# Joining the value products of two query tiles in a differential attention, with feature-major outputs and moved weight and gate splits

## The chip, the cores and the metric

The kernel runs on one core of a Trainium2 chip. The metric is the device time of one execution in microseconds. A core has a matrix engine (TensorE, PE in the profile, with its weight loads as PEld), a vector engine (VectorE, DVE), an engine for activations (ScalarE, ACT), a general one (GpSimd, POOL) and one that issues transfers (SP). Each takes its instructions in the order of its own queue and waits where an operand or a buffer isn't ready.

## What is computed

The reference is a block of two layers over 1024 latent tokens with 256 context tokens, 1024 features. The even layer has a Fourier mixer and a differential attention side by side, the odd layer a gated short convolution. The part that the change is about is the attention of the even layer and what follows it:

```python
def one_block(qblk):
    s = jnp.einsum('bqhmd,bkhmd->bhmqk', qblk, k,
                   preferred_element_type=jnp.float32) * ATTN_SCALE
    p = jax.nn.softmax(s, axis=-1)
    a = p[:, :, 0] - lam * p[:, :, 1]
    return jnp.einsum('bhqk,bkhv->bqhv', a.astype(v.dtype), v)
...
ao = (rms_norm(attn_o, subln_g) * (1.0 - lam_init)).reshape(b, n, ATT_WIDTH)
y = jnp.concatenate([fo, ao], axis=-1) * jax.nn.silu(proj[..., G0:])
return y @ w_out
```

There are 4 heads, each with two score maps over 1280 keys (context and latent), and values of 128 features. `rms_norm` divides by the root of the mean square over the 128 features of a token's output; a softmax's denominator that is common to both maps can be left out ahead of it, as long as the small constant in the norm is scaled with its square.

## The kernel before

All of it runs with the matrix engine as the main worker. Products that must be more exact than one pass are split: an operand is cast to a rounded high part (ScalarE) and the rest is subtracted as a low part (VectorE or POOL), and three products are summed.

**Projections** (lines 598 to 667). Tokens are taken in tiles of 128; `proj_tok` makes 24 records of 128x512 for one of them. `wnext(n)` splits the next n weight tiles (line 185, with `whalf`, lines 171 and 172) and asks for the next raw ones. Only TensorE's order is written out by hand in this stage; the other engines' is found by a scheduler.

**Fourier mixer and gates** (lines 749 to 953, TensorE and VectorE in written order). `fft_a(g)` makes the sequence transform of group g and splits its results (`split`, lines 744 and 746); `fft_b` transforms over channels and writes `fo` (line 789). Between them stand the gates' products. `tpart` makes split copies of `tk` for the gates in `arena`: line 885 is the high part on ScalarE, line 888 the low part on VectorE, and lines 866 and 867 first complete `tk` for the later quarters.

**Attention** (lines 1157 to 1205, all engines in written order). The 32 steps i are query tiles of 128 for (head, tile). For each of the two maps a score goes to its own three banks (S0, S1; lines 1025 and 1026); VectorE takes the row maximum (`rowmax`, line 1030), ScalarE the exponential with its row sum (`expo`, line 1041). `combine(i - 1)` forms p0 + cc * p1, 1024 keys on VectorE (line 1055), 256 on POOL (lines 1052, 1053). `turn(i - 2, c)` transposes up to four key blocks into a bank and ScalarE copies them out as `aT` (line 1067). `values(i - 2)` sums ten products with aT as the stationary operand and 128 value features as the moving one, so that the output lies token-major (line 1075); VectorE copies it to `o` (line 1084) and ScalarE sums its squares per token (line 1090).

Four tiles are a group g. `fin_a` has POOL turn the sums into 1/root (lines 1096 to 1100, the power at 1100) and scale `o` (1101). `fin_b` transposes the four outputs (1109), VectorE applies gain and gate to `y` (1111), ScalarE casts the high part (1113) and POOL subtracts for the low part (1115).

PSUM has eight banks. S0 and S1 hold six; the two others are the pool `pst` with its tag "t": `ps_t` (a turn), `ps_av` (values) and `ps_o` (outputs) take them in turn, and whoever comes next waits until the readers of the one before the last are done.

**End of the attention** (lines 1190 to 1205). The last two tiles' turns and values are put between the steps of the first output projections (`proj_feat2(W[0], 0)`, then W[1]; `at={k: ...}` names what goes ahead of step k; one step is three records of 512 columns).

Of the kernel before, what the change touches and what calls it, by code (L numbers as in the profile page):

```python
# [17 lines left out]
P = 128  # L18
# [19 lines left out]
def block_kernel(tc, A):  # L38
# [44 lines left out]
    ones_dv = const.tile([P, 1], F32, name="ones_dv")  # L83
    nc.vector.memset(ones_dv, 1.0 / P)
# [533 lines left out]
    for tt in range(NTC, NK):  # L618
        if tt == NTC + 1:
            wnext(2)  # L620
# [128 lines left out]
    def fft_a(g):  # L749
# [4 lines left out]
        for i in range(4):  # L754
# [303 lines left out]
    def turn(i, c):  # L1058

        n = min(4, NK - 4 * c)  # L1060
        pt = pst.tile([P, NB], F32, name="ps_t", tag="t", bufs=2)
        p0 = tiles[i, 0][0]
        for j in range(n):
            k = 4 * c + j
            nc.tensor.transpose(pt[:, j * P:(j + 1) * P], p0[:, k * P:(k + 1) * P], ident)  # L1065
        at = av.tile([P, NB], F32, name="aT", bufs=4)
        nc.scalar.copy(out=at[:, :n * P], in_=pt[:, :n * P])
        groups[i, c] = at

    def values(i):  # L1070
        g, j = divmod(i, 4)
        v = preps[i // 8][2]
        ps = pst.tile([P, NB], F32, name="ps_av", tag="t", bufs=2)[:, :P]
        for k in range(NK):
            nc.tensor.matmul(ps, lhsT=groups[i, k // 4][:, (k % 4) * P:(k % 4 + 1) * P],  # L1075
                             rhs=v[:, k * P:(k + 1) * P], start=k == 0, stop=k == NK - 1)
# [7 lines left out]
        nc.vector.tensor_copy(out=o[:, j, :], in_=ps)

    def squares(i):
        g, j = divmod(i, 4)
        o, ss, _ = groups[g, "f"]
        sq = av.tile([P, P], F32, name="osq", bufs=1)
        nc.scalar.activation(out=sq, in_=o[:, j, :], func=AF.Square, accum_out=ss[:, j:j + 1])  # L1090

    def fin_a(g, eng=nc.gpsimd):

        o, ss, _ = groups[g, "f"]
        z0 = z0s.pop(g)
        nc.gpsimd.tensor_tensor(out=z0, in0=z0, in1=z0, op=ALU.mult)
        nc.gpsimd.tensor_scalar(out=z0, in0=z0, scalar1=EPS, scalar2=None, op0=ALU.mult)
        nc.gpsimd.tensor_scalar(out=ss, in0=ss, scalar1=1.0 / DV, scalar2=None, op0=ALU.mult)
        nc.gpsimd.tensor_tensor(out=ss, in0=ss, in1=z0, op=ALU.add)
        nc.gpsimd.tensor_tensor(out=ss, in0=ss, in1=mhalf[:, 0:4], op=ALU.pow)  # L1100
        eng.tensor_tensor(out=o, in0=o, in1=ss.unsqueeze(2).broadcast_to([P, 4, P]), op=ALU.mult)

    def fin_b(g):

        f, half = NH + g // 2, g % 2
        o, _, sg = groups.pop((g, "f"))
        pt = pst.tile([P, NB], F32, name="ps_o", tag="t", bufs=2)
        for j in range(4):
            nc.tensor.transpose(pt[:, j * P:(j + 1) * P], o[:, j, :], ident)
        y = av.tile([P, NB], F32, name="y", bufs=1)  # L1110
        nc.vector.scalar_tensor_tensor(out=y, in0=pt, scalar=g08, in1=sg, op0=ALU.mult, op1=ALU.mult)
# [45 lines left out]
    for i in range(NQ):  # L1157
        if i % 8 == 0 and i // 8 + 1 < NH:
            loads = att_prep(i // 8 + 1, nc.sync)
        if i % 8 > 1:  # L1160
            for _ in range(min(3, len(loads))):
                loads.pop(0)()
        score(i, 0)
        if i >= 2:
            turn(i - 2, 0)
            turn(i - 2, 1)
# [3 lines left out]
        if i >= 3:  # L1170
            squares(i - 3)
        if i >= 6 and i % 4 == 2:
            fin_a((i - 6) // 4)
# [6 lines left out]
        if i >= 2:  # L1180
            values(i - 2)
        if i >= 7 and i % 4 == 3:
            fin_b((i - 7) // 4)
# [14 lines left out]
    pend = [proj_feat2(W[0], 0, {1: lambda: turn(NQ - 2, 2), 2: lambda: values(NQ - 2), 4: lambda: turn(NQ - 1, 0),  # L1198
                                 5: lambda: (turn(NQ - 1, 1), squares(NQ - 2)), 7: lambda: turn(NQ - 1, 2)})]
    values(NQ - 1)  # L1200
    squares(NQ - 1)
    fin_a(NG - 1, nc.vector)
    pend.append(proj_feat2(W[1], 0))
# [558 lines left out]
```

## Time and profile before

| what | us |
|---|---|
| median of 3 runs | 1080.52 (1079.1 to 1081.81) |
| the profiled execution | 1081.25 |
| its span | 1079.4 |
| attention, from the first exponential of the first tile to that of the last | 371.62 to 554.74 |
| busy: PE, DVE, ACT, POOL | 1031.8, 760.0, 480.7, 436.8 |

The profile comes from one execution. Its span reaches from the first to the last instruction of the program; the execution's time has something around it. Durations of matrix records overlap with those of their neighbours, so their pace is read from starts or from the chain of waits, which follows what ended last back from the end of the program. In the timeline a row's end tells in brackets how long the engine was idle before it and what ended that.

### The profile page before, as it was taken

The numbers are of one execution on the slowest core, as the hardware profiler recorded it, in microseconds if no ns is written. First come the engines' busy times: TensorE is split into PE (matmuls) and PEld (weight loads), VectorE is DVE, ScalarE is ACT, GpSimd is POOL, SyncE is SP. The second block draws the span as 40 slices with busy tenths as digits, with TensorE's granted clock in tenths as the row PEclk, the third lists the DMA queues.
The fourth block names the chain that finished last, engine by engine and source line by source line (L and its number), as shares of the span: only waits on it lengthen the run. The fifth ranks groups of instructions, "written<-read, shape, count | busy, mean of one in ns | idle before, by whom it ended". The sixth has DMA issues, their size and how long they took to land.

```text
span 1079.4 us, 14123 instructions
## 1 busy us (share of the span) xinstructions
PE 1031.8 (96%) x5128; PEld 843.3 (78%) x5128; DVE 760.0 (70%) x1112; ACT 480.7 (45%) x876; POOL 436.8 (40%) x379
## 2 busy tenths in 40 slices
PE   6989999989999899999999999999999999998898
PEld 3667888878887699899988878777888888786676
DVE  4599956957888288888873386996555554579953
ACT  4453234312445377777763363634333333343420
POOL 1257115530454047775666644034443543402031
PEclk9999999999999999999999999999999999998999
DMA  9823896354111987081004643021112111113421
GB/s 335 339 97 117 253 370 225 108 152 136 43 61 66 249 196 177 25 190 52 18 21 156 198 156 134 0 78 60 59 39 75 43 60 59 59 39 107 145 99 58
DMA packets 61380, 131.12 MB, mean 121 GB/s; under 512 B 5248, under 2 KB 30208, under 8 KB 58112
## 3 DMA queue, kind: packets, MB, share of 16 engines
q1 hardware_dynamic: 60240, 125.64, 36.7%
q0 software_dynamic: 1072, 4.59, 1.2%
q8 instruction: 40, 0.66, 0.3%
q14 instruction: 28, 0.23, 0.1%
HBM read 105.57 MB, written 24.64 MB: 121 GB/s over the span
## 4 chain that ended last, share of the span: by engine, by line
PE 64%; DVE 21%; POOL 4%; ACT 4%; issue 3%; DMA 3%; SPq 0%; ACTq 0%; POOLq 0%; DVEq 0%
PE psX L657 6%; PE psX L659 6%; PE psX L658 6%; PE ps_av L1075 5%; PE ps_tok L284 3%; PE ps_tok L285 3%; PE ps_tok L286 3%; PE psY L658 3%; PE psY L659 3%; PE psY L657 3%; PE S L1025 3%; PE S L1026 3%; DVE nm L1030 2%; PE ps_t L1065 2%; DMA ada_raw<-in_ada_dram 2%
## 5 line engine op out<-in xcount | busy, mean ns | idle before, releaser
L284 PE MATMUL ps_tok<-whi,hhi 128*128 128x512 f32 x288 | 118.0, 410 | 2.5 <-ACT hhi L393 1.5
L285 PE MATMUL ps_tok<-whi,hlo 128*128 128x512 f32 x288 | 115.0, 399 | 3.5 <-DVE hlo L397 3.5
L286 PE MATMUL ps_tok<-wlo,hhi 128*128 128x512 f32 x288 | 114.8, 399 | 0.6 <-DVE wlo L172 0.4
L634 POOL TENSOR_TENSOR s<-wraw 128x512 f32<-128x512 f32 x20 | 26.7, 1333 | 212.5 <-DMA wraw<-in_wodd_dram 101.7
L1030 DVE TENSOR_REDUCE nm<-S 128x1 f32<-128x1280 f32 x64 | 95.2, 1487 | 22.0 <-PE S L1026 17.2
L1041 ACT ACTIVATE p<-S,nm 128x1280 f32<-128x1280 f32 x64 | 85.1, 1330 | 44.7 <-DVE nm L1030 40.9
L61 ACT CAST wop<-wraw 128x512 fp32r<-128x512 f32 x106 | 65.2, 619 | 82.7 <-PE ps_feat L1130 22.0
L657 PE MATMUL psX<-B,wop 128*128 128x512 f32 x240 | 95.6, 398 | 5.0 <-ACT u L1366 2.5
L659 PE MATMUL psX<-B,wop 128*128 128x512 f32 x240 | 95.3, 397 | 4.3 <-DVE wop L1312 4.3
L658 PE MATMUL psX<-B,wop 128*128 128x512 f32 x240 | 94.8, 395 | 0.0
L62 POOL TENSOR_TENSOR wop<-wraw,wop 128x512 fp32r<-128x512 f32 x52 | 71.5, 1377 | 42.1 <-ACT wop L61 42.0
L1075 PE MATMUL ps_av<-v,aT 128*128 128x128 f32 x640 | 76.8, 276 | 0.0
L1075 PEld LDWEIGHTS ps_av<-v,aT 128*128 128x128 f32 x640 | 74.2, 192 | 0.2
L285 PEld LDWEIGHTS ps_tok<-whi,hlo 128*128 128x128 f32 x288 | 55.1, 191 | 16.8 <-DVE hlo L397 6.0
L284 PEld LDWEIGHTS ps_tok<-whi,hhi 128*128 128x128 f32 x288 | 55.3, 192 | 16.2 <-issue 2.2
L1052 POOL TENSOR_TENSOR p<-p,cc 128x256 f32<-128x256 f32 x32 | 40.3, 1259 | 64.7 <-DVE cc L1049 45.1
L286 PEld LDWEIGHTS ps_tok<-wlo,hhi 128*128 128x128 f32 x288 | 55.1, 191 | 13.1 <-DVE wlo L172 1.4
L658 PE MATMUL psY<-B,wop 128*128 128x512 f32 x160 | 63.6, 397 | 1.7 <-DVE B L1259 1.7
L659 PE MATMUL psY<-B,wop 128*128 128x512 f32 x160 | 63.5, 397 | 0.0
L657 PE MATMUL psY<-B,wop 128*128 128x512 f32 x160 | 63.5, 397 | 0.0
L657 PEld LDWEIGHTS psX<-B,wop 128*128 128x128 f32 x240 | 45.1, 188 | 18.3 <-ACT u L1366 3.4
L659 PEld LDWEIGHTS psX<-B,wop 128*128 128x128 f32 x240 | 45.0, 188 | 17.0 <-DVE wop L1312 6.2
(354 smaller groups left out, 2694.5 us busy)
## 6 DMA issues: line engine op xcount, KB each, us to landing
ada_raw<-in_ada_dram SPq DMA_DIRECT2D x24, 1024.0 KB, 7.6
wraw<-in_wodd_dram SPq DMA_DIRECT2D x32, 512.0 KB, 3.5
wraw<-in_wo_dram SPq DMA_DIRECT2D x24, 512.0 KB, 4.1
wraw<-in_wtok_dram SPq DMA_DIRECT2D x16, 512.0 KB, 5.3
arena<-kd SPq DMA_DIRECT2D x16, 320.0 KB, 9.0
kq<-kd SPq DMA_DIRECT2D x16, 320.0 KB, 10.2
xt<-in_xT_dram SPq DMA_DIRECT2D x16, 256.0 KB, 6.3
xr<-in_xT_dram SPq DMA_DIRECT2D x16, 256.0 KB, 4.0
```

What stands on the lines that cost most here:

```text
L61: nc.scalar.copy(out=o[:, 0, :], in_=src)
L62: eng.tensor_tensor(out=o[:, 1, :], in0=src, in1=f32(o[:, 0, :]), op=ALU.subtract)
L284: nc.tensor.matmul(ps, lhsT=hh, rhs=whi, start=k == 0, stop=False)
L285: nc.tensor.matmul(ps, lhsT=hl, rhs=whi, start=False, stop=False)
L286: nc.tensor.matmul(ps, lhsT=hh, rhs=wlo, start=False, stop=k == KT - 1)
L657: nc.tensor.matmul(ps, lhsT=a, rhs=x[k][0], start=start and k == 0, stop=False, skip_group_check=not start)
L658: nc.tensor.matmul(ps, lhsT=a, rhs=x[k][1], start=False, stop=False, skip_group_check=not start)
L659: nc.tensor.matmul(ps, lhsT=b, rhs=x[k][0], start=False, stop=k == 3, skip_group_check=not start)
L1030: nc.vector.tensor_reduce(out=nm, in_=S[m][:, :NKEY], op=ALU.max, axis=AX.X, negate=True)
L1041: nc.scalar.activation(out=p, in_=S[m][:, :NKEY], func=AF.Exp, bias=tiles.pop((i, m, "nm")), accum_out=z)
L1052: nc.gpsimd.tensor_tensor(out=p1[:, ks], in0=p1[:, ks], in1=c.broadcast_to([P, POOLK]), op=ALU.mult)
L1075: nc.tensor.matmul(ps, lhsT=groups[i, k // 4][:, (k % 4) * P:(k % 4 + 1) * P], rhs=v[:, k * P:(k + 1) * P], start=k == 0, stop=k == NK - 1)
```

## The change

1. **Two tiles in one product.** With i odd, a = i - 3 is the first of two tiles that are handled together; in the next, even step a is the same. `turn(a, c)` transposes key blocks 2c and 2c + 1 of both tiles into one bank; five turns make 512 columns each. `values(a, keys)` has the values as the stationary operand and 256 columns of aT as the moving one, so the output is feature-major, 128 features by 256 tokens. Turns 0 and 1 stand in the odd step behind the first score, turns 2 and 3 behind the second; turn 4 and key blocks 0 to 3 in the even step behind the first score, blocks 4 to 9 behind the second. The last two tiles' turns and values stand in the first output projection.
2. **Norm and gate, feature-major.** `outputs` has VectorE scale by the gain, a number for each partition now, and ScalarE square, both out of PSUM, for two tiles at once. `fin_z` and `fin_a` (POOL) do the small constant and the gate. `fin_m` sums squares over features with four one-column products, `fin_d` makes 1/root and a diagonal of it, `fin_r` spreads it over all partitions with a product of 512 columns, and `fin_b` multiplies. The gain now carries the root of 128 in place of a mean.
3. **Weight splits.** `wnext(2)` in the query loop becomes `wnext(1)` at two tiles.
4. **Gates' low parts.** In the last `fft_a` the first quarter's `tpart` goes ahead of the splits.
5. A constant that nothing read is gone.

The diff, without renamed comments and blank lines:

```diff
-        nc.vector.tensor_scalar(out=g08, in0=small[:, S_SUB:S_SUB + 1], scalar1=1.0 - LAM0, scalar2=None,
+        nc.vector.tensor_scalar(out=g08, in0=small[:, S_SUB:S_SUB + 1], scalar1=(1.0 - LAM0) * DV ** 0.5, scalar2=None,
...
-        if tt == NTC + 1:
-            wnext(2)
+        if tt in (NTC + 1, NTC + 3):
+            wnext(1)
...
-    def fft_a(g):
+    def fft_a(g, then=None):
...
+        if then:
+            then()
         ch, cl = split(fev, pc, NB, "gc", 1)
...
-    cur = fft_a(3)
+    qs = [quarter_of(t) for t in arena]
+    cur = fft_a(3, lambda: tpart(qs[0], range(4)))
     gate_product(1, 1)
     gop(1, 2)
-    qs = [quarter_of(t) for t in arena]
-    tpart(qs[0], range(4))
     fft_b(*cur)
...
+    def turn(a, c):
         pt = pst.tile([P, NB], F32, name="ps_t", tag="t", bufs=2)
+        for n in range(4):
+            k, p0 = 2 * c + n // 2, tiles[a + n % 2, 0][0]
+            nc.tensor.transpose(pt[:, n * P:(n + 1) * P], p0[:, k * P:(k + 1) * P], ident)
+        at = av.tile([P, NB], F32, name="aT", bufs=5)
+        nc.scalar.copy(out=at, in_=pt)
+    def values(a, keys):
+        v = preps[a // 8][2]
+        if keys[0] == 0:
+            groups[a, "ps"] = pst.tile([P, NB], F32, name="ps_av", tag="t", bufs=2)[:, :2 * P]
+        for k in keys:
+            nc.tensor.matmul(groups[a, "ps"], lhsT=v[:, k * P:(k + 1) * P],
+                             rhs=groups[a, k // 2][:, (k % 2) * 2 * P:(k % 2 + 1) * 2 * P], start=k == 0,
+                             stop=k == NK - 1)
+    def outputs(a):
...
+        nc.vector.tensor_scalar(out=o[:, qs], in0=ps, scalar1=g08, scalar2=None, op0=ALU.mult)
+        nc.scalar.activation(out=sq[:, qs], in_=ps, func=AF.Square)
+    def fin_z(g):
+        z0 = z0s[g]
+        nc.gpsimd.tensor_tensor(out=z0, in0=z0, in1=z0, op=ALU.mult)
+        nc.gpsimd.tensor_scalar(out=z0, in0=z0, scalar1=EPS * DV, scalar2=None, op0=ALU.mult)
     def fin_a(g, eng=nc.gpsimd):
+        o, _, sg = groups[g, "f"]
+        eng.tensor_tensor(out=o, in0=o, in1=sg, op=ALU.mult)
+    def fin_m(g):
+        ps, sq, z0 = pst.tile([P, NB], F32, name="ps_m", tag="t", bufs=2)[:, :4], groups[g, "f"][1], z0s.pop(g)
+        for j in range(4):
+            nc.tensor.matmul(ps[:, j:j + 1], lhsT=sq[:, j * P:(j + 1) * P], rhs=ones[:, 0:1], start=True, stop=True)
+    def fin_d(g):
+        nc.vector.tensor_tensor(out=z0, in0=ps, in1=z0, op=ALU.add)
+        nc.gpsimd.tensor_tensor(out=z0, in0=z0, in1=mhalf[:, 0:4], op=ALU.pow)
+        dg = groups[g, "d"] = av.tile([P, 4, P], F32, name="dg", bufs=1)
+        nc.gpsimd.tensor_tensor(out=dg, in0=ident.unsqueeze(1).broadcast_to([P, 4, P]),
+                                in1=z0.unsqueeze(2).broadcast_to([P, 4, P]), op=ALU.mult)
+    def fin_r(g):
+        ps = groups[g, "r"] = pst.tile([P, NB], F32, name="ps_o", tag="t", bufs=2)
+        nc.tensor.matmul(ps, lhsT=ones, rhs=groups.pop((g, "d")).rearrange("p j d -> p (j d)"), start=True, stop=True)
     def fin_b(g):
+        nc.vector.tensor_tensor(out=y, in0=groups.pop((g, "r")), in1=y, op=ALU.mult)
...
+        odd, a = i % 2, i - 3 - (i + 1) % 2
         score(i, 0)
+        if a >= 2 and odd:
+            outputs(a - 2)
+        if a >= 0 and odd:
+            turn(a, 0)
+            turn(a, 1)
+        elif a >= 0:
+            turn(a, 4)
+            values(a, range(0, 4))
         rowmax(i, 0)
...
         score(i, 1)
+        if a >= 0 and odd:
+            turn(a, 2)
+            turn(a, 3)
+            if a >= 4 and a % 4 == 0:
+                fin_m((a - 4) // 4)
+            elif a >= 6:
+                fin_r((a - 6) // 4)
+        elif a >= 0:
+            values(a, range(4, NK))
         rowmax(i, 1)
+        if a >= 4 and a % 4 == 0 and odd:
+            fin_d((a - 4) // 4)
+        if a >= 6 and a % 4 == 2 and odd:
+            fin_b((a - 6) // 4)
         expo(i, 1)
...
+    turn(NQ - 4, 4)
+    values(NQ - 4, range(NK))
+    fin_r(NG - 2)
+    fin_b(NG - 2)
+    outputs(NQ - 4)
     combine(NQ - 1)
+    pend = [proj_feat2(W[0], 0, {2: lambda: turn(NQ - 2, 0), 3: lambda: turn(NQ - 2, 1),
+                                 4: lambda: turn(NQ - 2, 2), 5: lambda: turn(NQ - 2, 3),
+                                 6: lambda: turn(NQ - 2, 4)})]
+    values(NQ - 2, range(NK))
+    outputs(NQ - 2)
     fin_a(NG - 1, nc.vector)
+    pend.append(proj_feat2(W[1], 0, {2: lambda: (fin_m(NG - 1), fin_d(NG - 1)), 7: lambda: fin_r(NG - 1)}))
```

How the instructions stand now is shown at three places. First ScalarE in the attention, before: one step, with `p0` and `p1` the exponentials of the two maps, `aT` the copies of turned weights, `osq` the squares.

```order
L1067 COPY aT_3375<-ps_t_3370 128x512
L1067 COPY aT_3382<-ps_t_3377 128x512
L1090 ACTIVATE osq_3392,ss_3294<-o_3293 128x128
L1041 ACTIVATE p0_3394,z0_3395<-S0_3166,nm0_3384 128x1280
L1067 COPY aT_3406<-ps_t_3403 128x256
L1041 ACTIVATE p1_3410,z1_3411<-S1_3167,nm1_3408 128x1280
```

And the same place now, an odd step and the even one behind it:

```order
L1089 ACTIVATE osq_3388<-ps_av_3459 128x256
L1064 COPY aT_3506<-ps_t_3501 128x512
L1064 COPY aT_3513<-ps_t_3508 128x512
L1040 ACTIVATE p0_3524,z0_3349<-S0_3164,nm0_3515 128x1280
L1064 COPY aT_3537<-ps_t_3532 128x512
L1064 COPY aT_3544<-ps_t_3539 128x512
L1040 ACTIVATE p1_3557,z1_3558<-S1_3165,nm1_3551 128x1280
L1064 COPY aT_3571<-ps_t_3566 128x512
L1040 ACTIVATE p0_3586,z0_3587<-S0_3164,nm0_3578 128x1280
L1040 ACTIVATE p1_3603,z1_3604<-S1_3165,nm1_3601 128x1280
```

The odd step has four copies now, two of them behind its first exponential, and the even step one.

Second, TensorE in the same steps, before, without the records of the scores (`ps_t` a turn, `ps_av` the values, `ps_o` the output's transposes):

```order
L1065 MATMUL ps_t_3853<-cst_78,p0_3736 128x128 x4
L1065 MATMUL ps_t_3860<-cst_78,p0_3736 128x128 x4
...
L1065 MATMUL ps_t_3885<-cst_78,p0_3736 128x128 x2
L1075 MATMUL ps_av_3895<-v1_3168,aT_3858 128x128 x4
L1075 MATMUL ps_av_3895<-v1_3168,aT_3865 128x128 x4
L1075 MATMUL ps_av_3895<-v1_3168,aT_3888 128x128 x2
L1109 MATMUL ps_o_3907<-cst_78,o_3567 128x128 x4
```

Now, from the second score of an odd step to the first values of the even one, again without the scores; of each turn only the first transpose of each tile is shown:

```order
L1062 MATMUL ps_t_3532<-cst_78,p0_3348 128x128
L1062 MATMUL ps_t_3532<-cst_78,p0_3415 128x128
...
L1062 MATMUL ps_t_3539<-cst_78,p0_3348 128x128
L1062 MATMUL ps_t_3539<-cst_78,p0_3415 128x128
...
L1106 MATMUL ps_m_3546<-ones_80,osq_3388 128x1
...
L1062 MATMUL ps_t_3566<-cst_78,p0_3348 128x128
L1062 MATMUL ps_t_3566<-cst_78,p0_3415 128x128
...
L1073 MATMUL ps_av_3573<-aT_3506,v0_2076 128x256 x2
L1073 MATMUL ps_av_3573<-aT_3513,v0_2076 128x256 x2
```

The third bank that an odd step asks for behind its first turns is now that of ps_m (or ps_o), ahead of the next step's first score.

Third, VectorE at the end of the attention, before, from the last maximum (`o<-ps_av` the output copies, `y` a group's output, `p` the combination, `x` an output of W[0]):

```order
L1030 TENSOR_REDUCE nm_5234<-S_3167 128x1
L1084 COPY o<-ps_av 128x128
L1111 SCALAR_TENSOR_TENSOR y<-ps_o,g_102,sga 128x512
L1048 RECIPROCAL cc<-z_5237 128x1
L1049 SCALAR_TENSOR_TENSOR cc<-cc,neglam,z_5031 128x1
L1055 SCALAR_TENSOR_TENSOR p_5221<-p_5236,cc,p_5221 128x1024
```

And now:

```order
L1111 TENSOR_TENSOR z_4546<-ps_m,z_4546 128x4
L1125 TENSOR_TENSOR o<-ps_o,o 128x512
L1088 TENSOR_SCALAR o<-ps_av,g_100 128x256
L1047 RECIPROCAL cc<-z_4973 128x1
L1048 SCALAR_TENSOR_TENSOR cc<-cc,neglam,z_4774 128x1
L1054 SCALAR_TENSOR_TENSOR p_4939<-p_4972,cc,p_4939 128x1024
```

The last tile's combination stands behind the output of group 6, which needs `fin_r`, and behind the outputs of tiles 28 and 29.

More of the change, by code (lines that the diff above doesn't have):

```diff
@@ L82, in block_kernel @@
     nc.vector.memset(mhalf, -0.5)
-    ones_dv = const.tile([P, 1], F32, name="ones_dv")
-    nc.vector.memset(ones_dv, 1.0 / P)
     xs = [[None] * KT for _ in range(2)]
@@ L1056, in combine @@
                                        op1=ALU.add)
-    def turn(i, c):
-        n = min(4, NK - 4 * c)
+    def turn(a, c):
         pt = pst.tile([P, NB], F32, name="ps_t", tag="t", bufs=2)
[L1062 to L1076, printed above, removed]
+        for n in range(4):
+            k, p0 = 2 * c + n // 2, tiles[a + n % 2, 0][0]
+            nc.tensor.transpose(pt[:, n * P:(n + 1) * P], p0[:, k * P:(k + 1) * P], ident)
@@ new lines, in turn @@
+        at = av.tile([P, NB], F32, name="aT", bufs=5)
+        nc.scalar.copy(out=at, in_=pt)
+        groups[a, c] = at
+    def values(a, keys):
[6 more added lines that the diff above has]
+                             stop=k == NK - 1)
@@ L1077, in values @@
+    def outputs(a):
+        g, j = divmod(a, 4)
         if j == 0:
-            o = av.tile([P, 4, P], F32, name="o", bufs=2)
-            ss = av.tile([P, 4], F32, name="ss", bufs=2)
+            o = av.tile([P, NB], F32, name="o", bufs=2)
+            sq = av.tile([P, NB], F32, name="osq", bufs=1)
             sg = av.tile([P, NB], F32, name="sga", bufs=2)
             nc.sync.dma_start(out=sg, in_=sgd[g // 2, :, (g % 2) * NB:(g % 2 + 1) * NB])
-            groups[g, "f"] = [o, ss, sg]
-        o, ss, _ = groups[g, "f"]
@@ L1084, in values @@
[L1084 to L1090, printed above, removed]
-    def fin_a(g, eng=nc.gpsimd):
[L1094 to L1101, printed above, removed]
+            groups[g, "f"] = [o, sq, sg]
@@ new lines, in outputs @@
+        o, sq, _ = groups[g, "f"]
+        ps, qs = groups.pop((a, "ps")), slice(j * P, (j + 2) * P)
+        nc.vector.tensor_scalar(out=o[:, qs], in0=ps, scalar1=g08, scalar2=None, op0=ALU.mult)
[4 more added lines that the diff above has]
+        nc.gpsimd.tensor_scalar(out=z0, in0=z0, scalar1=EPS * DV, scalar2=None, op0=ALU.mult)
+    def fin_a(g, eng=nc.gpsimd):
+        o, _, sg = groups[g, "f"]
+        eng.tensor_tensor(out=o, in0=o, in1=sg, op=ALU.mult)
@@ L1103, in fin_b @@
+    def fin_r(g):
+        ps = groups[g, "r"] = pst.tile([P, NB], F32, name="ps_o", tag="t", bufs=2)
+        nc.tensor.matmul(ps, lhsT=ones, rhs=groups.pop((g, "d")).rearrange("p j d -> p (j d)"), start=True, stop=True)
     def fin_b(g):
         f, half = NH + g // 2, g % 2
[L1106 to L1110, printed above, removed]
@@ L1111, in fin_b @@
-        nc.vector.scalar_tensor_tensor(out=y, in0=pt, scalar=g08, in1=sg, op0=ALU.mult, op1=ALU.mult)
+        y, _, _ = groups.pop((g, "f"))
+        nc.vector.tensor_tensor(out=y, in0=groups.pop((g, "r")), in1=y, op=ALU.mult)
         yh = yao.tile([P, NB], F32R, name="yh", tag="y", bufs=16)
@@ L1169, in block_kernel @@
             combine(i - 1)
[L1170 to L1173, printed above, removed]
+        if a >= 4 and a % 4 == 0 and odd:
+            fin_a((a - 4) // 4)
+        if a >= 2 and a % 4 == 2 and not odd:
+            fin_z((a - 2) // 4)
         expo(i, 0)
         score(i, 1)
-        if i >= 2:
-            turn(i - 2, 2)
+        if a >= 0 and odd:
[7 more added lines that the diff above has]
+            values(a, range(4, NK))
         rowmax(i, 1)
+        if a >= 4 and a % 4 == 0 and odd:
+            fin_d((a - 4) // 4)
+        if a >= 6 and a % 4 == 2 and odd:
+            fin_b((a - 6) // 4)
         expo(i, 1)
[L1180 to L1183, printed above, removed]
         if i == 4:
@@ L1189, in block_kernel @@
             fo_split(*fo, i // 4 - 2, nc.gpsimd)
-    turn(NQ - 2, 0)
-    turn(NQ - 2, 1)
+    turn(NQ - 4, 4)
[3 more added lines that the diff above has]
+    outputs(NQ - 4)
     combine(NQ - 1)
-    squares(NQ - 3)
+    fin_z(NG - 1)
     cls("sco")
@@ L1197, in block_kernel @@
     y0(0)
[L1198 to L1201, printed above, removed]
+    pend = [proj_feat2(W[0], 0, {2: lambda: turn(NQ - 2, 0), 3: lambda: turn(NQ - 2, 1),
[3 more added lines that the diff above has]
+    outputs(NQ - 2)
     fin_a(NG - 1, nc.vector)
-    pend.append(proj_feat2(W[1], 0))
+    pend.append(proj_feat2(W[1], 0, {2: lambda: (fin_m(NG - 1), fin_d(NG - 1)), 7: lambda: fin_r(NG - 1)}))
     w0next(eng=nc.vector)
```

5 lines of the change are left out of this document (2 added, 3 removed).

## The prediction

> **What bounds the kernel now.** I read the page's first part, then the attention stage in windows and in the chain of waits, because nearly all edits lie there. First the page's engine totals and the row of the stage in the view by windows (busy us, instructions, granted clock, DMA share, GB/s).
>
> ```profile
> PE 1031.8 (96%) x5128; PEld 843.3 (78%) x5128; DVE 760.0 (70%) x1112; ACT 480.7 (45%) x876; POOL 436.8 (40%) x379
> 388.50:554.70 166.20, 163.69 (x1202) 151.45 (x1201) 142.85 (x175) 125.89 (x264) 104.86 (x116) 1.00 0.38 94
> ```
>
> TensorE is busy 98% of this stage at full clock. VectorE, at 86%, has some slack. So the question is what TensorE gets to do, and whether it then has to wait. The chain (start, us, what) has one query tile in it:
>
> ```profile
> 498.67 0.23 PE S L1025
> ...
> 499.71 0.12 PE S L1026
> 499.83 0.87 PE ps_t L1065 x8
> ...
> 501.86 0.22 PE ps_t L1065 x2
> 502.08 2.23 PE ps_av L1075 x20
> 504.31 0.23 PE S L1025
> ```
>
> A score is 4x0.23 + 2x0.12 = 1.16 us; with eight transposes, the second score, two transposes and the 20 records of the value product the tile takes 504.31 - 498.67 = 5.64 us. Where VectorE and ScalarE end last, the chain reads so:
>
> ```profile
> 488.00 0.13 PE S L1026
> ...
> 488.23 1.49 DVE nm L1030
> ...
> 490.08 1.74 DVE p L1055
> 491.81 1.41 DVE nm L1030
> ...
> 493.31 0.95 ACT p L1041
> ...
> 494.78 0.50 PE S L1025
> ```
>
> From the end of a score, 488.13, its maximum starts 0.10 later and lasts 1.49; the weights' combination starts 1.85 after that start and lasts 1.74 here (1.28 elsewhere in the chain, with POOL quiet); the second maximum, 1.41, ends at 493.22, the exponential starts at 493.31, and the next score in that bank starts 1.47 later. The starts of the first exponentials give the real pace (timeline; the rows are those of tiles 1, 2, 3, 7 and 31):
>
> ```profile
> 377.21 1.33 ACT L1041 ACTIVATE p<-S,nm 128x1280 f32<-128x1280 f32 x1 [1.28 <-DVE nm L1030]
> 382.51 1.35 ACT L1041 ACTIVATE p<-S,nm 128x1280 f32<-128x1280 f32 x1
> 388.52 1.32 ACT L1041 ACTIVATE p<-S,nm 128x1280 f32<-128x1280 f32 x1
> 411.95 1.33 ACT L1041 ACTIVATE p<-S,nm 128x1280 f32<-128x1280 f32 x1
> 554.74 1.33 ACT L1041 ACTIVATE p<-S,nm 128x1280 f32<-128x1280 f32 x1
> ```
>
> From tile 7 to tile 31 it is 142.79 / 24 = 5.95, so **11.90 us for two tiles**, of which 11.28 are the work above and 0.22 a group's output transposes.
>
> **The change, part by part.** What do the new TensorE operations cost? A stream of 256-column f32 records is not in the trace. Its neighbours are (TensorE's timeline, start and us; then the row of line 228 with ns min/median/max, and the page's group of the value products, busy us and mean ns):
>
> ```profile
> 137.90 0.39 PE L286 MATMUL ps_tok<-wlo,hhi 128*128 128x512 f32 x1
> 138.13 0.95 PE L591 MATMUL ps_col<-ones,ada_sum 128*128 128x1 f32 x8
> 139.25 0.39 PE L285 MATMUL ps_tok<-whi,hlo 128*128 128x512 f32 x1
> 624.15 0.39 PE L1130 MATMUL ps_feat<-yh,wop 128*128 128x512 f32 x1
> 624.38 1.02 PE L228 MATMUL ps_r<-dg,ones 128*128 128x512 f32 x2
> 625.47 0.40 PE L1129 MATMUL ps_feat<-yfo,wop 128*128 128x512 f32 x1
> L228 PE MATMUL ps_r<-dg,ones x10: 379/592/1055, 17.0 to 668.0; 128*128 128x512 f32 x8, 128*128 128x256 f32 x2
> L1075 PE MATMUL ps_av<-v,aT 128*128 128x128 f32 x640 | 76.8, 276 | 0.0
> ```
>
> Between the starts either side stand two ordinary records (0.23 each) and the odd ones. So eight one-column records take 1.35 - 0.46 = 0.89 us, 0.11 each, and two 512-column records 1.32 - 0.46 = 0.86, 0.43 each. A 128-column record takes 2.23/20 = 0.11 as well: up to 128 columns something other than streaming sets the pace. For 256 columns the ends are 0.11, as for 1 and 128, and 0.43, as for 512. I take half of 512's, **0.215**, because the durations grow with the columns as a streamed length would: 276 ns for 128, 379 for 256 (the shortest of line 228), 592 for 512.
>
> So 20 records for two tiles take 4.30 instead of 2 x 2.23 = 4.46: **the joined product saves only 0.16 us a pair.** Feature-major output removes four transposes a group (two of them took 0.22, so 0.44) and adds fin_m, the 0.89, and fin_r, the 0.86. In all TensorE gets (0.89 + 0.86)/2 - 0.22 - 0.16 = +0.5 us more for each pair. VectorE and ScalarE are relieved (one copy and one square for two tiles, no accumulator reads, five copies of 512 instead of six), but they weren't the main bound.
>
> Then the order. I walk one pair, 0 being the start of the odd tile's first score. Odd: score 1.16, eight transposes to 2.03, score to 3.19, eight transposes to 4.06. Now fin_m or fin_r wants a bank of the two-bank ring "t", the one that holds the third turn; this must first be copied by ScalarE, whose queue has that copy behind the first exponential. The maximum runs 1.26 to 2.75, the exponential starts at 2.83, and then:
>
> ```profile
> 493.31 1.33 ACT L1041 ACTIVATE p<-S,nm 128x1280 f32<-128x1280 f32 x1 [1.72 <-DVE nm L1030]
> ...
> 494.63 1.06 ACT L1067 COPY aT<-ps_t 128x512 f32<-128x512 f32 x2
> ```
>
> The copies start 1.32 after the exponential, at 4.15, the first is done at about 4.74, and fin starts near 4.8: **a wait of 0.74 that every odd tile from 7 on gets, with the whole TensorE queue behind it**, the next tile's first score above all, though that could go at 4.30 (2.83 + 1.47). Fin ends at 5.67. Even: score 1.16, four transposes 0.44, eight value records 1.72, score 1.16, twelve value records 2.58: 7.05. The pair takes **12.7 us**. VectorE's second maximum of the odd tile ends by 6.2, its exponential by 7.7, before the score that needs it at 9.0, so they hide.
>
> Twelve such pairs (tiles 7 to 30): 12 x (12.7 - 11.9) = **+9.7** (unrounded 0.81). Tiles 3 to 6 have no fin: two pairs of 4.30 + 7.05 = 11.35 against 388.52 to 411.95, **-0.7**. Tile 2 has no turn any more and goes at the pace of tile 1, 5.30 instead of 6.01: **-0.7**. Bounds: without any wait, 12.0 a pair, the three come to -0.2; with the output's cast ahead of the exponential in every second pair (y 0.75, cast 0.61, exponential at 7.7 to 9.2 against 9.0) they are about +10.
>
> **The tail.** What tile 2 saved comes back here. Now, from the start of tile 31's first score to W[2]'s first record (chain, then timeline), with the operations that move:
>
> ```profile
> 551.79 0.23 PE S L1025
> 577.35 0.40 PE L1128 MATMUL ps_feat<-yfo,wop 128*128 128x512 f32 x1
> 552.97 1.04 POOL L1100 TENSOR_TENSOR ss<-ss,mhalf 128x4 f32<-128x4 f32 x1
> 554.08 1.04 POOL L1101 TENSOR_TENSOR o<-o,ss 128x512 f32<-128x512 f32 x1
> 557.77 2.51 POOL L1151 TENSOR_TENSOR yfo<-arena,yfo 128x512 fp32r<-128x512 f32 x2
> 558.28 0.74 DVE L1111 SCALAR_TENSOR_TENSOR y<-ps_o,g,sga 128x512 f32<-128x512 f32 x1
> ```
>
> That is 25.5. After: 4.06 and fin_m to 5.7, turn to 6.1, the bank of fin_m from fin_d at about 6.4, ten value products to 10.7, fin_r to 11.6 (POOL's gain, power and diagonal, 1.04 each, are through by then). VectorE has y (to 12.4) and the outputs copy (12.8) ahead of tile 31's combination, which ends near 14.7; TensorE has done two steps of W[0] by 13.0 and **waits some 1.7 us at tile 31's first turn**. Six steps (0.70 each) and five turns bring it to 21.2, ten value products to 25.5, W[1] with fin_m and fin_r to 5.6 + 1.75 more, 32.8. So **+7.3**; work alone, without these waits, gives +4.4, and a POOL that is late with the diagonal +8.6.
>
> **The gates' low parts.** Here VectorE waits, and later TensorE waits for it (timeline; the last row is from the list of waits):
>
> ```profile
> 305.57 0.15 DVE L792 COPY fo<-mid 128x1 f32<-128x1 f32 x1
> 307.91 0.69 DVE L746 TENSOR_TENSOR gcl<-ps_gc,gch 128x512 fp32r<-128x512 f32 x1 [2.18 <-ACT gch L744]
> 309.78 3.59 DVE L888 TENSOR_TENSOR arena<-tk,arena 128x512 fp32r<-128x512 f32 x4
> 313.29 1.28 DVE L789 TENSOR_TENSOR fo<-v,ps_fo 128x512 f32<-128x512 f32 x2
> PE psX L659 <- DVE gop L62: 2.2, 1, 2.2
> ```
>
> The four low parts move into the idle 2.18. The products behind them then start at about 312.2, when the copy v is there, not 313.29. The 2.2 wait gets shorter by **1.1**; bounds 0 (POOL slows VectorE) and 2.2. The split weight calls leave every engine's instructions up to there in the old order: **0**, and nothing to hide.
>
> **Sum:** 9.7 - 0.7 - 0.7 + 7.3 - 1.1 = +14.5. The profiled execution took 1081.25, its span 1079.4 and 1.85 around it; its median stands 0.7 lower. So 1095.75 by the profile, and 1080.52 + 14.5 = **1095** by the runs.
>
> **Rivals.** *Faster: the wide product goes at the pace of a narrow one.* 1 and 128 columns take the same 0.11, so a fixed cost covers at least 128; if it covers 256 too, a pair's values take 2.24, not 4.30, 16 x 2.06 = 33 us go, and the time is 1062. It decides below about 0.17 a record (14.5/320 less than 0.215). Against it speak the 0.43 at 512 and the growing durations. 5%. [...]
>
> *The waits are hidden,* since another bank comes free or the copy comes earlier: 12 x 0.72 + 0.7 = 9.4 less, 1086. For it speaks VectorE's slack; against it the queue order of ScalarE. 20%. *The waits breed more,* with exponentials behind the output's cast and POOL late at the end: some 4 us on top, 1099. 10%. *The edit does nothing:* so it is for the weight calls, with no effect on the sum; for the rest the order rules it out. *Forecast,* 1090 to 1098: 60%. Nothing of these, to either side: 5%.
>
> **Range and chances.** From the hidden case to the deeper one with their bounds, **1084 to 1101**, which leaves out the fast rival and stray cases, some 12%. A measurement here tells about 0.3%, 3.2 us, from no change. Faster by more 0.06, within it 0.05, slower by more 0.89.
>
> **What would show it.** Right: value products of 256 columns 0.21 to 0.22 apart; a gap of about 0.7 ahead of ps_m and ps_o in every odd tile, released by ScalarE; first exponentials 12.7 apart for two tiles; W[2]'s first record near 33 us after tile 31's first score; the wait on the gates' low part at 1.1. Wrong: no gap there, or a pace of records near 0.11.

## The result, and the profile after

| | before | after |
|---|---|---|
| median of 3 runs, us | 1080.52 (1079.1 to 1081.81) | 1096.02 (1095.96 to 1096.46) |
| profiled execution, us | 1081.25 | 1095.96 |
| its span, us | 1079.4 | 1093.8 |

The ratio is 1.0132, with a 95% interval from 1.0107 to 1.0156: slower, by 15.5 us, where +14.5 had been forecast. The sum came out nearly exactly. Its terms did not all do so, and the experiments show that one edit which got no price at all, the constant, gave back 5 to 6 us in a stage that the sum had left at 0.

First the engine totals of the changed kernel, from its page.

```profile
PE 1036.8 (95%) x4856; PEld 842.0 (77%) x4856; DVE 752.7 (69%) x1103; ACT 478.7 (44%) x812; POOL 443.6 (41%) x371
```

TensorE has 272 records fewer than before (4856, 5128) and is busy 5 us longer. Its new operations are in the view by groups (line, operation, tiles, shape, count; busy us and mean ns of one; idle time just before and what ended it):

```profile
L1073 PE MATMUL ps_av<-aT,v 128*128 128x256 f32 x320 | 74.1, 379 | 0.0
...
L1120 PE MATMUL ps_o<-dg,ones 128*128 128x512 f32 x16 | 8.6, 620 | 4.5 <-ACT aT L1064 4.5
L1106 PE MATMUL ps_m<-ones,osq 128*128 128x1 f32 x64 | 8.3, 251 | 4.7 <-ACT aT L1064 4.7
```

Fin_m and fin_r have 9.2 us of waiting ahead of them, and what ends it is ScalarE's copy of a turn. The timeline has the first exponentials of tiles 1, 2, 3, 7 and 31 again:

```profile
377.90 1.33 ACT L1040 ACTIVATE p<-S,nm 128x1280 f32<-128x1280 f32 x1 [1.19 <-DVE nm L1029]
383.09 1.33 ACT L1040 ACTIVATE p<-S,nm 128x1280 f32<-128x1280 f32 x1 [0.73 <-DVE nm L1029]
388.48 1.35 ACT L1040 ACTIVATE p<-S,nm 128x1280 f32<-128x1280 f32 x1
411.71 1.33 ACT L1040 ACTIVATE p<-S,nm 128x1280 f32<-128x1280 f32 x1
567.73 1.33 ACT L1040 ACTIVATE p<-S,nm 128x1280 f32<-128x1280 f32 x1
```

From tile 7 to tile 31 it is 156.02 / 12 = **13.00 us a pair**, against 11.90 before and 12.7 in the forecast. One pair in the chain of waits (start, us, what):

```profile
499.94 0.23 PE S L1024
...
501.21 1.50 DVE nm L1029
...
502.73 0.90 ACT p L1040
...
504.07 0.57 ACT aT L1064
504.63 0.14 issue
504.77 1.10 PE ps_o L1120 x2
505.87 0.23 PE S L1024
...
507.03 0.44 PE ps_t L1062 x4
507.47 1.73 PE ps_av L1073 x8
...
510.37 2.59 PE ps_av L1073 x12
512.96 0.23 PE S L1024
```

Score, maximum, exponential, the copy of the third turn behind it, and only then fin_r, 4.83 after the odd tile's first score. The value products take 2.59 / 12 = 0.216 us each. Last, TensorE's timeline at the places where the stages meet: the first score, the first score of tile 31, the wait in the tail, and, at the end, two records of the output projections.

```profile
369.44 0.39 PE L1024 MATMUL S<-arena 128*128 128x512 f32 x1
...
564.58 0.58 PE L1024 MATMUL S<-kq 128*128 128x512 f32 x1
...
580.35 0.55 PE L1062 MATMUL ps_t<-cst,p 128*128 128x128 f32 x3 [2.37 <-DVE p L1054]
...
596.72 0.39 PE L1142 MATMUL ps_feat<-yfo,wop 128*128 128x512 f32 x1
...
597.40 0.39 PE L1142 MATMUL ps_feat<-yfo,wop 128*128 128x512 f32 x1
```

The last row, at 597.40, is the 49th record of the output projections, as W[2]'s first one, at 577.35, is in the kernel before; the stretches are cut there. In the changed kernel W[2] starts a little earlier, at 596.72: the built program puts its first five steps ahead of fin_r of the last group (which starts at 600.16) and of W[1]'s last step. So this fin_r falls into the last stretch.

And the first score of the kernel before:

```profile
368.65 0.39 PE L1025 MATMUL S<-arena 128*128 128x512 f32 x1
```

With these and the rows of before, the 14.4 us between the spans fall into four stretches:

| stretch | before | after | difference | forecast |
|---|---|---|---|---|
| start to the first score | 368.65 | 369.44 | +0.8 | -1.1 |
| first score to tile 31's first score | 182.9 | 195.1 | +12.2 | +8.3 |
| from there to the 49th record of the output projections | 25.8 | 32.8 | +7.0 | +7.3 |
| from there to the end | 502.0 | 496.4 | -5.6 | 0 |

So the loop was under-priced by 4 us, and 5.6 us came back in a stage that the change hardly touches, although fin_r's 0.86 stands in it now. (The first score of tile 31 before starts at 551.55.)

### The profile page after: what moved, and what is told of

Read it like the earlier page. It is cut to its first block, busy times and chain, and to the rows that moved or that the text cites. A ratio compares the mean times of both kernels' runs of the same rounds, so it can differ in the third digit from the quotient of the medians.

```text
span 1093.8 us, 13456 instructions
## 1 busy us (share of the span) xinstructions
PE 1036.8 (95%) x4856; PEld 842.0 (77%) x4856; DVE 752.7 (69%) x1103; ACT 478.7 (44%) x812; POOL 443.6 (41%) x371
## 4 chain that ended last, share of the span: by engine, by line
PE 66%; DVE 19%; ACT 6%; issue 4%; POOL 4%; DMA 2%; SPq 0%; ACTq 0%; DVEq 0%; POOLq 0%
PE psX L655 6%; PE ps_av L1073 6%; PE psX L657 6%; PE psX L656 6%; PE ps_tok L282 3%; PE ps_tok L283 3%; PE ps_tok L284 3%; PE psY L657 3%; PE psY L655 3%; PE psY L656 3%; PE S L1024 3%; PE S L1025 3%; PE ps_feat L1144 2%; PE ps_feat L1143 2%; ACT p L1040 2%
## 5 line engine op out<-in xcount | busy, mean ns | idle before, releaser
L62 POOL TENSOR_TENSOR wop<-wraw,wop 128x512 fp32r<-128x512 f32 x52 | 75.5, 1454 | 34.5 <-ACT wop L61 34.5
L1051 POOL TENSOR_TENSOR p<-p,cc 128x256 f32<-128x256 f32 x32 | 48.5, 1515 | 83.4 <-PE S L1025 48.0
L1073 PE MATMUL ps_av<-aT,v 128*128 128x256 f32 x320 | 74.1, 379 | 0.0
L1073 PEld LDWEIGHTS ps_av<-aT,v 128*128 128x128 f32 x320 | 58.5, 190 | 6.9
```

The source lines that it names most:

```text
L62: eng.tensor_tensor(out=o[:, 1, :], in0=src, in1=f32(o[:, 0, :]), op=ALU.subtract)
L1051: nc.gpsimd.tensor_tensor(out=p1[:, ks], in0=p1[:, ks], in1=c.broadcast_to([P, POOLK]), op=ALU.mult)
L1073: nc.tensor.matmul(groups[a, "ps"], lhsT=v[:, k * P:(k + 1) * P], rhs=groups[a, k // 2][:, (k % 2) * 2 * P:(k % 2 + 1) * 2 * P], start=k == 0,
```

## Experiments

**Where do the 5.6 us at the end come from?** From the first output projection on, most of TensorE's records are weight products of 512 columns, the same ones in both kernels. In the kernel before they start 0.2333 us apart, in the changed one 0.2292. The one edit that reaches this stage is the constant that nothing read: it takes 4 bytes a partition, rounded up to 32 in the built program, and all tiles behind it on the left side of the memory, the weight tiles among them, lie 32 bytes lower without it. Five kernels move that boundary and nothing else; a sixth is the unchanged kernel.

`const_back`, the changed kernel with the constant:

```diff
     nc.vector.memset(mhalf, -0.5)
+    ones_dv = const.tile([P, 1], F32, name="ones_dv")
+    nc.vector.memset(ones_dv, 1.0 / P)
```

> The changed kernel with the unread constant ones_dv (4 bytes a partition, 32 with its rounding) put back; all else as changed. Question: from the first output projection on, the changed kernel's 512-column records follow each other every 0.2292 us, those of the kernel before every 0.2333, and 5.6 us come back between W[2]'s first record and the end. Theory 'address': the constant moves everything on the left side of the on-chip memory by 32 bytes; without it the moving and the stationary operands both start at 32 modulo 64, with it one of them at 0 and the other at 32, and such a pair costs about 4 ns a record. Then the late step goes back to 0.2333 and the time rises by 5 to 8 us, to 1101 to 1104. Rival 'attention': the later gain comes from the other pools or buffers of the attention, or from the state of the chip in that run; then the late step stays at 0.229 and the time at 1096.

`const_gone`, the kernel before without it:

```diff
-    ones_dv = const.tile([P, 1], F32, name="ones_dv")
-    nc.vector.memset(ones_dv, 1.0 / P)
```

> The kernel before with only the unread constant ones_dv taken out. Theory 'address': the late step goes from 0.2333 to 0.2292 and the time falls by 5 to 8 us, to 1072.5 to 1075.5. Rival 'attention': 0.2333 and 1080.5, no change.

`const_nine` and, later, `const_seventeen`, the kernel before with a wider one:

```diff
-    ones_dv = const.tile([P, 1], F32, name="ones_dv")
+    ones_dv = const.tile([P, 9], F32, name="ones_dv")
```

> The kernel before with the constant ones_dv nine numbers wide instead of one: it takes 64 bytes a partition instead of 32, so that what lies behind it moves by 32 bytes the other way. Theory 'address, modulo 64': as without the constant, a late step of 0.229 and 1072.5 to 1075.5. Rival 'room' (what counts is the memory or the instruction that is saved, or a distance other than modulo 64): 0.2333 and 1080.5 or slower.

> The kernel before with the constant seventeen numbers wide (96 bytes a partition, so what lies behind it moves by 64 bytes). Theory 'address': moving and stationary operand differ by 224 modulo 256 instead of 32, again an odd multiple of 32; the late step stays at 0.233 and the time at 1079 to 1083, though the constant is larger than in the run with nine. Rival 'a wider constant is faster for another reason': a step of 0.227 to 0.229 and 1070 to 1075.

`before_again`, the kernel before:

> The kernel before, unchanged, for its trace on this chip: how much the pace and the start-up differ from run to run. Both theories: 1079 to 1082, a late step of 0.2333; if the step is 0.229 here, the pace belongs to the chip or the run and not to the kernel.

`after_pad`, the changed kernel with 64 bytes more:

```diff
     nc.vector.memset(mhalf, -0.5)
+    pad = const.tile([P, 9], F32, name="pad")
+    nc.vector.memset(pad, 0.0)
```

> The changed kernel with a pad of 64 bytes a partition among the constants and nothing else. Moving and stationary operand then start at the same place modulo 256 instead of 64 apart. Theory 'address': the late step falls from 0.2292 to 0.2271, the time by some 4 us to 1090 to 1093; the attention's pair stays at 13.0. Rival: only the 32-byte place matters; 0.2292 and 1096.

The view by windows counts TensorE's records in 100 us of the last stage, all of them busy (the fourth figure is the count). Before:

```profile
780.00:880.00 100.00, 100.00 (x430) 80.51 (x429) 53.46 (x82) 35.46 (x61) 43.81 (x32) 1.00 0.16 53
```

The changed kernel:

```profile
800.00:900.00 100.00, 100.00 (x438) 81.95 (x437) 53.99 (x82) 36.45 (x62) 44.91 (x34) 1.00 0.15 53
```

`const_gone`:

```profile
780.00:880.00 100.00, 100.00 (x438) 81.90 (x438) 51.57 (x82) 36.15 (x61) 46.63 (x34) 1.00 0.16 53
```

`const_nine`:

```profile
770.00:870.00 100.00, 100.00 (x443) 82.81 (x442) 53.57 (x85) 37.35 (x63) 43.98 (x32) 1.00 0.17 58
```

`const_seventeen`:

```profile
780.00:880.00 100.00, 100.00 (x431) 80.57 (x430) 54.10 (x87) 36.31 (x61) 41.21 (x30) 1.00 0.17 58
```

All at full granted clock; nothing but the spacing differs. Set beside the addresses of the built programs, where "apart" is the start of the moving operand minus that of the stationary one which the next record brings, modulo 256 bytes (spacing: mean of the 1900 to 2000 late records with both neighbours of 512 columns; time: median, or the one run):

| kernel | apart | spacing, ns | time, us | ratio to before, its interval |
|---|---|---|---|---|
| before_again | 32 | 233.3 | 1080.14 | one run |
| const_back | 32 | 233.4 | 1101.23 | 1.0183 (1.0153 to 1.0213) |
| const_seventeen | 224 | 233.3 | 1084.51 | one run |
| after | 64 | 229.2 | 1096.02 | 1.0132 (1.0107 to 1.0156) |
| const_gone | 64 | 229.2 | 1075.22 | 0.994 (0.9921 to 0.9959) |
| const_nine | 0 | 227.1 | 1070.16 | 0.9896 (0.9859 to 0.9932) |
| after_pad | 0 | 227.0 | 1093.09 | one run |

The theory of the address holds at every point, the rivals at none: putting the constant back costs the changed kernel its late gain, taking it away or widening it to nine gives the old kernel one, and seventeen, though larger, give none (its one run, 1084.5, lies above the 1079 to 1083 expected, but within the 1077.7 to 1086.9 of 17 runs of the kernel before). Nine came out better than expected (0.2271, not 0.229), which is how the third class, 0 against 64, was found; `after_pad` then met its forecast, 0.2271, in the changed kernel.

In all these kernels nearly all late moving operands start at the same place modulo 256 (224), so the stationary operand's own start might be what counts. It isn't: in the kernel before, stationary operands that start at 192 took 228.1 ns a record ahead of the attention, where the moving ones start at 192 too, and 233.3 late, where the moving ones start at 224.

The late stage's 2000 records by 4.1 ns are 8.2 us. Of these the changed kernel shows 5.6. Its late stretches of half clock, told of below, last 10.2 us together, those of the kernel before 6.8, which takes some 1.6 back; fin_r's 0.86 in place of four transposes of 0.43 takes another 0.4. The 0.6 left over is less than the 2.1 by which this stretch differs between two executions of the kernel before (502.1 and 499.9).

So **the change as such**, at the addresses of the kernel before, is const_back's 1.0183: about +20 us, not +15.5.

**The wait for the bank in the loop.** `fin_late` moves fin_m and fin_r behind the even step's value products, where the bank they ask for has long been free; fin_d and fin_b go to the start of the next odd step:

```diff
             outputs(a - 2)
+        if a >= 6 and a % 4 == 2 and odd:
+            fin_d((a - 6) // 4)
+        if a >= 8 and a % 4 == 0 and odd:
+            fin_b((a - 8) // 4)
...
             turn(a, 3)
-            if a >= 4 and a % 4 == 0:
-                fin_m((a - 4) // 4)
-            elif a >= 6:
-                fin_r((a - 6) // 4)
+            if i == NQ - 1:
+                fin_m((a - 4) // 4)
         elif a >= 0:
             values(a, range(4, NK))
+            if a >= 4 and a % 4 == 0:
+                fin_m((a - 4) // 4)
+            elif a >= 6:
+                fin_r((a - 6) // 4)
         rowmax(i, 1)
-        if a >= 4 and a % 4 == 0 and odd:
+        if i == NQ - 1:
             fin_d((a - 4) // 4)
-        if a >= 6 and a % 4 == 2 and odd:
-            fin_b((a - 6) // 4)
```

> The changed kernel with fin_m and fin_r moved from the end of the odd step to the end of the even one, behind all value products, and with fin_d and fin_b at the start of the next odd step; there the bank that they ask for is that of the fifth turn, copied long before. The work is the same. Theory 'bank': the gap of 0.76 us ahead of fin_m and fin_r goes, and the 0.24 that the products took on top behind the gap; a pair falls from 13.0 to 12.1 to 12.3 us and the time by 8 to 11 us, to 1085 to 1088. Rival 'chain': VectorE and ScalarE set the 13.0 us, or y ahead of the maximum costs as much as it saves; then the gap turns up elsewhere in the pair and the time stays within 2 us of 1096.

Measured: 1093.53 us, a ratio of 1.01 (1.0067 to 1.0133) to the kernel before, on a chip on which that took 1083.76. The start-ups of two executions differ by more than the effect, so the stretch from the first score to tile 31's is better: 190.0 against 195.1, 5.1 less, and 12.59 us a pair between tiles 7 and 31. The chain of this kernel, one pair:

```profile
506.56 0.86 PE ps_o L1120 x2
507.42 0.23 PE S L1024
...
508.69 1.50 DVE nm L1029
...
510.21 0.89 ACT p L1040
...
511.44 0.20 ACT p L1040
511.69 0.50 PE S L1024
...
519.28 0.79 PE ps_m L1106 x8
520.06 0.34 PE S L1024
```

The gap ahead of fin is gone, and in the stream fin_r takes 0.86, as had been reckoned, and fin_m 0.79 (0.89 reckoned), not the 1.10 and 1.05 of behind the gap. But TensorE now waits a little for the exponential that frees the even tile's score bank (511.44 + 0.20, then the score), and the first record after that wait takes 0.50 instead of 0.23. Of the 0.7 to 0.9 us expected a pair, 0.41 came. Both theories had a part: the bank's wait is real, and half of what it costs is taken over by the chain behind it. (In the tail this execution has a stretch of half clock, a granted clock of 0.90 on the mean from 569.1 to 585.4, and takes 34.7 us instead of 32.8.)

`fin_out` leaves fin's products out:

```diff
+        if g < NG - 2:
+            groups[g, "r"] = groups.pop((g, "d")).rearrange("p j d -> p (j d)")
+            return
         ps = groups[g, "r"] = pst.tile([P, NB], F32, name="ps_o", tag="t", bufs=2)
...
+        if g < NG - 2:
+            groups[g, "m"] = groups[g, "f"][1][:, :4], z0s.pop(g)
+            return
```

> The changed kernel without TensorE's products of fin_m and fin_r for the first six groups (their results are replaced by other data, so the norm of these groups is left out); fin_d and fin_b stay. What fin costs with its wait: theory 'bank' has 0.76 + 1.10 minus what the next score then waits for; a pair falls from 13.0 to 11.3 to 11.5, the time by about 18 us to 1078. If a pair stays above 11.8, something else waits there too.

One run, 1085.57 us; 12.06 us a pair, so the expected 11.3 to 11.5 was missed. TensorE's timeline in this kernel has one other wait, six times in the loop:

```profile
519.74 0.66 PE L1062 MATMUL ps_t<-cst,p 128*128 128x128 f32 x4 [0.56 <-ACT osq L1089]
```

And its chain has, in the pair ahead of that, the exponential as above:

```profile
508.75 0.90 ACT p L1040
509.65 0.33 issue
509.98 0.20 ACT p L1040
510.23 0.50 PE S L1024
```

With fin gone, a turn waits for the square of the outputs, whose bank it takes and which stands behind an exponential on ScalarE. Something waits for ScalarE in each of the three orders. Fin with its wait is worth 13.00 - 12.06 = 0.94 a pair, about its own work.

**The tail.** `tail_combine` puts the last tile's combination first:

```diff
+    combine(NQ - 1)
     turn(NQ - 4, 4)
     values(NQ - 4, range(NK))
     fin_r(NG - 2)
     fin_b(NG - 2)
     outputs(NQ - 4)
-    combine(NQ - 1)
```

> The changed kernel with the last tile's combination ahead of the output of group 6 and of the outputs of tiles 28 and 29 on VectorE. Theory: TensorE waits some 1.7 us at tile 31's first turn for this combination; from tile 31's first score to W[2]'s first record it then takes 31 instead of 32.8. Rival: the turn waits for a bank or the next operand anyway; 32.8 stays, or what is late moves to the outputs of tiles 28 and 29.

One run, 1090.34 us. From tile 31's first score to the 49th record of the projections it is 30.9 instead of 32.8, as expected. In its timeline the turns follow each other without a wait, and a small one has turned up at fin_r:

```profile
572.15 1.13 PE L1120 MATMUL ps_o<-dg,ones 128*128 128x512 f32 x2 [0.38 <-POOL dg L1114]
...
574.51 0.60 PE L1062 MATMUL ps_t<-cst,p 128*128 128x128 f32 x4
```

2.37 of waiting became 0.38: the 1.9 that was gained.

**The weight splits.** `before_wnext` is the old kernel with only this edit:

```diff
-        if tt == NTC + 1:
-            wnext(2)
+        if tt in (NTC + 1, NTC + 3):
+            wnext(1)
```

> The kernel before with only the weight splits apart (one weight tile at two query tiles instead of two at one). By the prediction 0, up to the gates. Rival: the 0.56 us that the changed kernel lost at the last query tile, where a product waits for a low part of the projection's input, come from this edit: then the same product starts 0.5 to 0.6 later here, against its neighbours.

1081.21 us in one run. From the 601st of the projections' records to the last it took 69.9 us, the kernel before 69.25 in one execution and 69.84 in the other: nothing that the same kernel doesn't show by itself. The changed kernel's 69.75 lies between them.

**Two versions that take the best of each.** `before_best` is the old kernel with nine numbers in the constant and the gates' low parts moved; `joined_best` has, beside the changed kernel's joined products, fin_late, tail_combine and the pad.

> The kernel before with the constant nine numbers wide and, of the change, only the gates' low parts ahead of the splits. Theory: nine numbers give 1070.2 against 1081.2 (0.2271 us a record late, against 0.2333), the moved low parts another 0.4 (the wait of TensorE on the gates' operand 1.8 instead of 2.2); together 1069 to 1071 where the kernel before has 1081, a ratio of 0.988 to 0.990. If the low parts gain nothing once the pace is faster, 0.990.

> The changed kernel with fin_m and fin_r at the end of the even step, the last tile's combination first in the tail, and a pad of 64 bytes a partition among the constants, so that the late operands start at the same place modulo 256. From the changed kernel's 1096: about -4.3 for the pad (2000 records by 0.0021), -5 for fin in the loop, -2 for the tail: 1083 to 1086 where the kernel before has 1081, a ratio of 1.002 to 1.005. That is, the joined products stay behind the plain kernel even so, since a pair keeps at least 11.35 of work plus 0.83 for fin against 11.9. Rival: with waits and tail mended it comes level or below: under 1081.

`before_best`: 1070.41 us, ratio 0.9883 (0.9852 to 0.9915), faster than both kernels. TensorE waits 1.9 for the gates' operand instead of 2.2; in the total the moved low parts can't be told from `const_nine` alone. `joined_best`: 1084.24 us, ratio 1.0017 (0.9998 to 1.0037), level with the kernel before as it was, and 14 us behind `before_best`, whose operands lie as far apart. Its pair still takes 12.59 us.

## Why the prediction was right, and where it wasn't

**The pace of the wide products: right.** 0.216 us a record against 0.215 forecast; the rival of the narrow pace fell. The remark that up to 128 columns something other than streaming sets the pace was too wide: half of 0.216 is 0.108, so that a record of 128 columns, at 0.11, takes no more than its share of columns. Only the one-column record, at 0.11 too, takes more.

**The wait in odd tiles: right in place, cause and size.** Fin starts 4.83 after the first score (4.8 forecast), the gaps ahead of ps_o and ps_m are 0.66 to 0.77 each, 8.6 us in the twelve odd tiles from 7 to 29, where 12 x 0.74 = 8.9 had been forecast (the 9.2 of the groups has tile 31's in it), and ScalarE's copy ends them. `fin_late` shows that it goes when the bank is another one.

**"Fin ends at 5.67": the term that was mis-sized.** After the gap fin takes 1.10 and 1.05, not 0.86 and 0.89. TensorE didn't resume at its pace here: the same products in the stream of `fin_late` took 0.86 and 0.79. Some 0.2 us in 12 pairs are 2.4 of the 3.5 us by which the loop's +13.2 exceeds +9.7; the rest is 0.04 in the even step (7.09, 7.05 forecast), 0.03 in the start and rounding. Tiles 3 to 6 gained 0.2, not 0.7. There the score comes behind the exponential, as in `fin_late`, where its first record took 0.27 more; twice that fits, but was not tried.

**"The waits are hidden": the price of this rival was wrong.** It took 0.72 a pair off. `fin_late` hid the wait and got 0.41, because the next wait stood close behind, the exponential that had been noted for the next score at 4.30.

**The tail: right in cause, +7.0 against +7.3, and in size partly by luck.** The combination behind the outputs makes TensorE wait at tile 31's first turn, as `tail_combine` shows. But the wait is 2.37 instead of 1.7: the combination took 2.32 us here, with POOL's low part (L1129, 1.24 us) and then its multiplication of the 256 keys (L1051, 1.12) beside it, and 1.28 in the loop, mostly with that multiplication alone beside it (1.18). POOL isn't quiet beside a short combination in the kernel before either: those of 1.28 have its multiplication beside them for 1.18 us, that of 1.74 has its multiplication for 0.61 and its addition (L1053) for 1.0. Against this stands fin_r, which the sum had at 0.86 ahead of W[2]'s first record and which comes behind the end of the stretch. The 25.5 of before was read from the second record of the score; from its first it is 25.8, and the 32.8 forecast for the changed kernel was met.

**"The products behind them then start ... when the copy v is there": wrong.** The wait for the gates' operand went from 2.2 to 1.8, by 0.4 instead of 1.1 (list of waits of the changed kernel, then its timelines of TensorE and VectorE):

```profile
PE psX L657 <- DVE gop L62: 1.8, 1, 1.8
```

```profile
313.78 0.40 PE L782 MATMUL ps_fo<-gsl,cht 128*128 128x512 f32 x1
...
314.37 1.29 DVE L789 TENSOR_TENSOR fo<-v,ps_fo 128x512 f32<-128x512 f32 x2 [2.49 <-ACT v L786]
```

VectorE is free 2.49 earlier, but its product needs ps_fo as well, whose last record starts at 313.78 and takes 0.40. The row names the copy v; TensorE's product was later.

**The weight calls: 0, right,** as far as this can be told.

**The constant: not in the sum at all.** It was told as an edit and never priced, since nothing reads it. It is worth 5.2 us in the changed kernel (1101.23 against 1096.02, in two sets of runs; by their ratios to the kernel before 5.5). Had its address been as before, the forecast of 1095.0 would have stood beside 1101. That the total was right is luck: the loop's 3.9 too little, the start's 1.9 and this -5.6 nearly cancel; of the start's, 0.7 is the gates' term and the rest is no more than two executions of the same kernel differ by (first score at 368.65 and at 370.42 before).

## What to carry to other kernels

A wait that a change removes is worth only the distance to the next one: look how far behind the second-latest releaser stands (here 0.41 of 0.72 a pair came), and add what the engine takes to resume (here 1.10 against 0.86 for fin_r). A join of two products pays only where two narrow records take longer than a wide one; here it was 2 x 0.11 against 0.216. And before a pace is compared between two kernels, compare where their operands lie: an edit of four bytes moved more here than several that were meant to.

## What the runs showed of the hardware

**Operand addresses.** With operands of the rounded type of the weight products, 512 moving and 128 stationary columns, the late back-to-back records took 227.1 ns where the two operands' starts are equal modulo 256 bytes (`const_nine`; `after_pad` 227.0), 229.2 where they are 64 apart (the changed kernel, `const_gone`) and 233.3 where they are 32 (`before_again`; `const_back` 233.4) or 224 apart (`const_seventeen`). The stages ahead of the attention in the kernel before have such classes side by side: a mean of 228 where the starts are equal, 231 to 233 where they are 32 or 224 apart. The scores of the attention, with equal starts, took 231 to 233, so the figures hold for the long streams of weight products and not for every stage. Why it is so stays open: the runs show the 6.2 ns a record between 227.1 and 233.3, and not what makes them.

**Half clock for some 3.4 us.** Now and then the granted clock falls to a half in these traces, mostly for 3.4 us or twice as long (0.50 from 1008.9 to 1012.3 in the changed kernel, 0.50 from 990.9 to 997.7 in the kernel before), and the records of 512 columns start 0.43 apart instead of 0.23. It isn't bound to a place in these runs: `const_gone` has it in the gates' stage (view by windows, the granted clock is the third figure from the end),

```profile
328.60:332.20 3.60, 3.60 (x11) 2.78 (x10) 3.53 (x5) 1.47 (x3) 2.09 (x2) 0.53 0.20 76
```

while the kernel before ran through the same products at full clock (1.00 from 326 to 368). The changed kernel has two such stretches late at places

```profile
736.20:739.80 3.60, 3.60 (x10) 2.86 (x10) 3.56 (x3) 1.37 (x3) 3.44 (x3) 0.58 0.00 0
1021.90:1025.70 3.80, 3.64 (x10) 2.81 (x11) 3.78 (x7) 2.55 (x6) 0.00 (x0) 0.59 0.53 180
```

where the kernel before is at full clock (1.00 from 716.0 to 719.6 and from 1007.4 to 1011.0); each costs 1.4 to 1.6 us, an estimate from the seven or eight records that stand 0.43 apart instead of 0.23. Both kernels have one behind a wait for a weight tile, of 3.79 us before and 3.84 in the changed kernel. There it lasts 3.4 us, from 1008.9, and in the kernel before twice as long:

```profile
990.90:997.70 6.80, 5.94 (x14) 4.38 (x15) 6.04 (x11) 1.14 (x2) 1.28 (x1) 0.50 0.32 111
```

Behind the tail's wait of 2.4 us `after_pad` shows one (0.90 on the mean of the stretch),

```profile
576.00:592.40 16.40, 14.04 (x67) 11.49 (x65) 3.70 (x5) 3.84 (x7) 9.07 (x11) 0.90 0.01 1
```

and the changed kernel, with the same wait, does not: a tail of 34.3 or of 32.8 us from the same code but for the pad. Behind the waits of 3.79 and 3.84 us both kernels had a stretch; the others here came behind waits of 2.08 to 2.36 us (2.29 in `const_gone`, 2.12 and 2.08 in the changed kernel, 2.36 in `after_pad`), in some executions and not in others. What sets one off was not shown. Some of the 9 us by which 17 runs of the kernel before differed (1077.68 to 1086.87) may be of this kind; it was not followed run by run.
